# An encoder trunk: gates and latent up-projections in alternation, one summed column in the first norm, one multiplication per settled head

## The chip, the core and the metric

The kernel runs on one core of a Trainium2 chip. A core has engines that work side by side, each through its own list of instructions in order: TensorE (PE) for matrix products, VectorE (DVE) and ScalarE (ACT) for work on elements, GpSimd (POOL), and SyncE (SP), which here issues the transfers (DMAs) from HBM into the on-chip memory (SBUF). Matrix products land in eight accumulation banks (PSUM). Engines wait for one another through semaphores. The metric is the time of one execution on the device in microseconds (us); lower is better.

## What is computed

Two layers of an encoder over 256 positions of width 2048, all in float32. Cut to the parts that the change touches:

```python
h = rmsnorm(x, g_mix[i])
z = h @ w_in[i]
dq, dk, dv, cq, ckv, kr, ga, gb = jnp.split(z, split_at, axis=-1)
# differential attention, 8 heads, two softmax maps each
od = diff_attention(dq, dk, dv, lam)
od = rmsnorm(od, g_subln[i], SUBLN_EPS) * (1.0 - lam_init)
y_diff = od.reshape(b, s, DIFF_WIDTH) @ w_branch_diff[i]
# latent attention, 8 heads
qf = (rmsnorm(cq, g_q_latent[i]) @ w_q_up[i]).reshape(b, s, MLA_HEADS, 192)
q_nope, q_rope = qf[..., :128], apply_rope(qf[..., 128:], cos_m, sin_m)
...
merged = jax.nn.sigmoid(ga) * y_diff + jax.nn.sigmoid(gb) * y_mla
x = x + merged @ w_out[i]
x = x + (silu(gate) * up) @ w_down[i]          # of rmsnorm(x) @ w_gate_up[i]
x = x + sigmoid(rmsnorm(x, g_ple[i]) @ w_ple_gate[i]) * e
```

`ga` and `gb` are the two gates, 2048 columns each. `cq` is the query latent of rank 512, from which `w_q_up` makes 8 heads of 128 plain columns and 64 rotated ones.

## The kernel before

**Products.** Activations are kept transposed, 128 features by 256 positions to a tile, and split into a high and a low part (`ua`, `ub`: 512 columns each). A weight comes by DMA as a piece of eight 128x128 blocks (`piece`, L198), is split into `whi` by ScalarE (L204) and `wlo` by VectorE (`tt`, L82), and for each block `emit` (L245) issues one product of 512 columns with `whi` (L254) and one of 256 columns with `wlo` (L255). `product` (L257) makes one output tile; with 16 blocks (a gate, a key, a query) it takes two pieces. `pair` (L268) makes two output tiles of four blocks each out of one piece: the up-projections. Each output tile takes one of the four banks of `ps_mm` in turn. `joined` (L277) empties a bank: ScalarE copies the right half (L279), VectorE adds the left half to it (L82, `a<-mm,join`). A bank can be used again when that addition is done.

**The order.** The Tile framework places the instructions on the engines with a simulated timeline, following the order in which the program issues them where their operands allow. A dependency of the kind `NO_SYNC` fixes an order on one engine without a semaphore. `after_splits` (L238) has what stands inside issued after the last weight split. `last_block` holds the last L255 product.

**The first norm** (L535 to L538). While x comes in, `squared` (L229) puts the squares of two feature tiles at a time beside each other into one [128, 2, 256] tile and adds these up in `sq0[0]` on VectorE. `norm` (L310) sums over the features with products against a column of ones (L315), one for each sum and half of the positions; with two sums these are four, in two records each. In the second layer it has one sum.

**The differential heads.** `pipelined` (L696) works through eight heads and calls `step` twice for each: 16 steps, each of which moves the generator `beside` (L614) on to its next `yield`. `beside` puts other products between the parts of a head: in steps 1 to 12 the remaining queries and keys, the key up-projections and `shared_key` (L396); in steps 13 to 16 the query up-projections 8, 0, 2 and 10 (8 and 10: the rotated parts of four heads each; 0 and 2: the plain parts of two heads each; two tiles each time), a gate behind 0 and behind 10; then two more gates. `queries_up` (L590) calls `pair` and, for plain parts, splits the joined tile (L288 or L289 on ScalarE, L85 on VectorE), for rotated parts calls `rotated` (L386): a shuffle (L381), two multiplications, an addition, and for each of two heads a conversion on ScalarE (L390) and a half on VectorE (L85). `gate` (L632) multiplies a joined product by the row factor `R`.

**The latent heads.** `pipelined` runs again with `some_gate` (L718) as its step: one gate in each, and ahead of it what `later` (L715) names for that step: the settling of heads 0 to 3 in step 0, `queries_up(4)` in step 2, the settling of heads 4 to 7 in step 4, `queries_up(6)` in step 7. Heads 4 to 7 read the rotated queries that `queries_up(10)` makes; the scores of head 4 are issued after step 6. `mla_weights` (L727) makes scores (L437), exponentials (L450) and normalised weights, `turned` (L454) transposes them (L459), `mla_out` (L736) multiplies with the values (L747).

**Settling** (`settle`, L685). The output of a differential head stands in `od[h]`, 128 positions by two blocks of 128 columns (one per block of positions). The inverse roots of the mean squares are taken for four heads at once (`rsqrt`, L291). Then for each block VectorE multiplies in place with the factor of its position (`ts`, L88) and PE transposes the block (L693).

Of the kernel before, what the change touches and what calls it, by code (L numbers as in the profile page):

```python
# [16 lines left out]
ALU = mybir.AluOpType  # L17
AX = mybir.AxisListType

P = 128  # L20
T = 256
DM = 2048
# [27 lines left out]
NO_SYNC = mybir.DependencyInfo(mybir.DependencyClass.NoSync, mybir.DependencyReason.DATA)  # L50
# [10 lines left out]
def encoder(ctx, tc, x, p, positions, cols, lams, wq, wk, wv, wcq, wckv, wkr, wga, wgb,  # L61
            w_q_up, w_kn, w_v, w_bd, w_bm, w_out, w_gate, w_up, w_down, w_pin, w_pg, w_pin_end, w_pg_end, g_end, rope_c, out):
    nc = tc.nc
    V, A, PE = nc.vector, nc.scalar, nc.tensor
# [13 lines left out]
    def bank(ps=ps_at, tag="at", name="at", shape=(P, 2 * T)):  # L78
        return ps.tile(list(shape), F32, tag=tag, name=name)

    def tt(o, a, b, op):
        return V.tensor_tensor(out=o, in0=a, in1=b, op=op)  # L82
# [4 lines left out]
    def ts(o, a, s1, s2, op0, op1=ALU.bypass):  # L87
        return V.tensor_scalar(out=o, in0=a, scalar1=s1, scalar2=s2, op0=op0, op1=op1)  # L88
# [11 lines left out]
    def operand(t):  # L100
        return t.rearrange("p c t -> p (c t)")
# [4 lines left out]
    def in_turn(u):  # L106
        return u.rearrange("p (c h t) -> p h t c", c=2, h=2)

    def by_parity(row):
        return row.rearrange("p (t c) -> p c t", c=2)  # L110
# [16 lines left out]
    ident = const.tile([P, P], F32, name="ident")  # L127
    make_identity(nc, ident)
    ones = const.tile([P, P], F32, name="ones")
# [99 lines left out]
    def squared(c):  # L229
        for j in range(c // 2, c // 2 + 2):  # L230
            sq0.append(fb(j))
            A.activation(sq0[j], xT[:, 2 * j : 2 * j + 2, :], AF.Square)
            if j:
                tt(sq0[0], sq0[0], sq0[j], ALU.add)

    last_split, last_mm, chores, sq0, step, last_block = [], [], [], [], [], [None]

    def after_splits():  # L238

        stack = ExitStack()  # L240
        for i in last_split:
            stack.enter_context(tc.issue_after(i.ins))
        return stack

    def emit(acc, hi, lo, at, us, first, last, whole):  # L245
        for j, u in enumerate(us):
            s, start, stop = slice((at + j) * P, (at + j + 1) * P), first and j == 0, last and j == len(us) - 1
            t = in_turn(u)
            if whole:
                PE.matmul(acc[:, :T], hi[:, s], t[:, 0], start=start, stop=False)  # L250
                PE.matmul(acc[:, :T], hi[:, s], t[:, 1], start=False, stop=False)
                PE.matmul(acc[:, :T], lo[:, s], t[:, 0], start=False, stop=stop)
            else:
                PE.matmul(acc, hi[:, s], t, start=start, stop=False)  # L254
                last_block[0] = PE.matmul(acc[:, T:], lo[:, s], t[:, 0], start=False, stop=stop)  # L255

    def product(src, us, whole=False):  # L257
# [10 lines left out]
    def pair(src, us):  # L268

        n = len(us)  # L270
        hi, lo = piece(src.rearrange("n p m -> p n m"), 2 * n)
        for j in range(2):
            acc = bank(ps_mm, "mm", "mm")
            emit(acc, hi, lo, j * n, us, True, True, False)
            yield acc

    def joined(acc, o=None):  # L277
        t = scratch("join", 3)
        A.activation(t, acc[:, T:], AF.Copy)  # L279
        o = scratch("a", 4) if o is None else o  # L280
        tt(o, acc[:, :T], t, ALU.add)
        return o
# [8 lines left out]
    def rsqrt(src, n, eps, width):  # L291

        v, y, a = (stat.tile([P, 2 * DH], F32, tag="r" + s, name="r" + s, bufs=2)[:, :width] for s in "vya")
        ts(v, src, 1.0 / n, eps, ALU.mult, ALU.add)
        ts(y.bitcast(I32), v.bitcast(I32), -0.5, 1597463007.0, ALU.mult, ALU.add)
        for _ in range(3):
            stt(a, y, -0.5, y, ALU.mult, ALU.mult)
            tt(a, a, v, ALU.mult)
            stt(y, a, 1.5, y, ALU.add, ALU.mult)
        return y  # L300
# [9 lines left out]
    def norm(sums, n):  # L310

        s = bank()
        for j, a in enumerate(sums):
            for b in range(2):
                PE.matmul(s[:, b : b + 1], by_parity(a)[:, b], ones[:, 0:1], start=j + b == 0, stop=j + b == len(sums))  # L315
        return rsqrt(s[:, 0:2], n, EPS, 2)

    def spread(col):

        s = bank()  # L320
        for b in range(2):
            PE.matmul(s[:, b * P : (b + 1) * P], col[:, b : b + 1].to_broadcast([P, P]), ident, start=True, stop=True)
        row = stat.tile([P, T], F32, tag="row", name="row", bufs=2)
        A.activation(row.rearrange("p (t c) -> p t c", c=2), s[:, :T].rearrange("p (c t) -> p t c", c=2), AF.Copy)
        return row
# [201 lines left out]
    for L in range(DEPTH):  # L527

        steps = values(wv[L], ua, None if L else load)
        for vd in steps:  # L530
            if L == 0 and vd is not None:
                chores.extend(lambda c=c: squared(c) for c in range(0, NC, 4))
                for _ in range(4):
                    next(steps)
                with after_splits():  # L535
                    rcol = norm([sq0[0][:, j, :] for j in range(2)], DM)
                    next(steps)
                    R = spread(rcol)  # L538
                    cos_p, sin_p, cos_m, sin_m = tables()
                    lambdas()  # L540
                break
            if L:
                next(steps)
                rcol = norm([acc], DM)
                next(steps)
                R = spread(rcol)
                break
# [42 lines left out]
        def queries_up(n):  # L590
            for acc in list(pair(w_q_up[L, n : n + 2], cq)):
                if n < MH:
                    qn.append(operand(fa(PLACES[len(qn)], F32R)))
                    split(qn[-1], joined(acc), MLA_SCALE)
                else:
                    if n > MH:
                        qr.append(operand(fc(len(qr) - 2, F32R)))
                    at = qr[len(qr) - 1] if n > MH else qr[ropes[0]]
                    rotated(joined(acc), cos_m, sin_m, at)
                    ropes[0] += 1  # L600
# [13 lines left out]
        def beside():  # L614

            for h in range(2, DH):
                queries_keys(h)
                yield
                if h < 6:
                    keys_up(2 * h - 4)  # L620
                elif h == 7:
                    shared_key(wkr[L], ua, crm, srm)
                yield
            for j, n in enumerate((8, 0, 2, 10)):
                queries_up(n)
                if j % 2:
                    gate(wga, gate_a, next(todo))
                yield
            for _ in range(2):
                gate(wga, gate_a, next(todo))  # L630

        def gate(w, store, n):  # L632
            tt(store(n), joined(product(w[L, n], ua)), R, ALU.mult)
# [12 lines left out]
        todo = iter(range(NC))  # L646
# [7 lines left out]
        od, ods, homes, last_out = [], ub[:8], [], [None]  # L654
# [30 lines left out]
        def settle(h0):  # L685

            rd = rsqrt(ssd[:, 2 * h0 : 2 * h0 + 8], P, SUB_EPS, 8)
            for h in range(h0, h0 + 4):
                t = bank()
                for b in range(2):  # L690
                    o, j = od[h][:, b * P : (b + 1) * P], 2 * (h - h0) + b
                    ts(o, o, rd[:, j : j + 1], None, ALU.mult)
                    PE.transpose(t[:, b * P : (b + 1) * P], o, ident)  # L693
                split(ods[h], t[:, :T], gsub[:, L : L + 1], blocks=True)

        def pipelined(weigh, put, heads, step):  # L696
# [15 lines left out]

        oms = ub[12:] + ub[8:12]
        ahead = iter(range(EARLY))
        later = {0: lambda: settle(0), 2: lambda: queries_up(4), 4: lambda: settle(4), 7: lambda: queries_up(6)}  # L715
        steps = itertools.count()

        def some_gate():  # L718
# [49 lines left out]
        acc, add = stream(ub, f"g_ffn{L}")  # L768
# [5 lines left out]
        R, _, pre = normed_rows(acc, lambda: product(w_gate[L, 0], ub), lambda: product(w_up[L, 0], ub))  # L774
# [5 lines left out]
        for part, (f0, f1) in enumerate(FF_PARTS):  # L780
            for f in range(f0, f1):
                a = pre.pop(0) if pre else joined(product(w_gate[L, f], ub))
                tt(a, a, R, ALU.mult)
                s = scratch("sig", 2)
# [3 lines left out]
                b = pre.pop(0) if pre else joined(product(w_up[L, f], ub))  # L788
# [3 lines left out]
            if last:  # L792
                acc, add = stream(ub, f"g_ple{L}")
# [8 lines left out]
            if part == 1 and L == DEPTH - 1:  # L802
# [7 lines left out]
                hi, lo = piece(w_pin_end, 8)  # L810
                for b in range(2):
                    acc_ = bank(ps_mm, "mm", "mmv")
                    for k in range(2):
                        s = slice(k * 512, (k + 1) * 512)
# [14 lines left out]
        else:  # L829
            acc, add = stream(ua, f"g_mix{L + 1}")  # L830
        for n in range(FM if final else NC):
            a = pre.pop(0) if pre else joined(product(w_pg[L * NC + n], ub))
            tt(a, a, R, ALU.mult)
            s = scratch("sig", 2)
# [4 lines left out]
            if final and n in (3, 5):  # L839
                b = (n - 3) // 2  # L840
                t = bank()
# [6 lines left out]
    for a in range(0, first, 2):  # L848
        m = min(2, first - a)
        hi, lo = piece(w_pg_end[:, a * 512 : (a + m) * 512], 4 * m)  # L850
        for j in range(m):
            s = slice(j * 512, (j + 1) * 512)
# [61 lines left out]
    for i in range(END - 1):  # L914
        o = fb(i).rearrange("p m (n t) -> p (m n) t", t=P)
# [11 lines left out]
    for i, queue in ((1, nc.sync), (0, nc.sync), (2, nc.scalar)):  # L927
        o = operand(fb(3 + i))
# [100 lines left out]
```

## Time and profile before

| what | before |
|---|---|
| median of 3 runs | 2720.53 us (2720.01 to 2720.70) |
| the profiled execution | 2720.81 us |
| its span in the trace | 2719.0 us |
| PE, DVE, ACT busy | 2706.3, 2064.6, 1570.1 us |
| first layer | 0 to about 1360 us |
| differential heads with their steps, first layer | about 106 to 215 us |
| latent heads, first layer | about 216 to 340 us |

All durations come from one profiled execution; the trace's span is 1.8 us shorter than the time of that execution on the device. An engine counts as busy while an instruction of it runs, and instructions of PE overlap, so the step from one start to the next tells more of its pace than the duration of one. A timeline row gives the start, the time taken, the engine, the line, the operation, the tile written and those read, and in square brackets the idle time before it and who ended it. In a row of groups stand the count, the busy time, the mean duration in ns, and the idle time of the engine before it. A row of waits gives who waited for whom, the total, the number and the longest. A row of windows gives the busy time of PE, of PE's weight loads, of DVE, ACT and POOL, the granted PE clock, and the DMA's share and rate.

### The profile page before, as it was taken

How to read it: one execution, taken by the hardware profiler on the slowest of the kernel's cores; microseconds unless marked ns; L12 is line 12 of the kernel's file. 1: busy time of each engine (PE TensorE's matmuls, PEld its weight loads, DVE VectorE, ACT ScalarE, POOL GpSimd, SP SyncE). 2: the span in 40 equal slices, each digit the busy share in tenths (PEclk: the TensorE clock that was granted, in tenths of full speed). 3: DMA queues.
4: the chain of work that ended last, by engine and by line, in shares of the span. 5: the costliest groups of instructions: out<-in, count | busy, mean ns of one | idle time of the engine just before them, and what ended most of it. 6: DMA issues, size and time to landing. Idle time of an engine off the chain costs nothing.

```text
span 2719.0 us, 43648 instructions
## 1 busy us (share of the span) xinstructions
PE 2706.3 (100%) x16608; PEld 2482.9 (91%) x16608; DVE 2064.6 (76%) x3426; ACT 1570.1 (58%) x2562; POOL 1.7 (0%) x9
## 2 busy tenths in 40 slices
PE   9999999999999999999999999999999999999998
PEld 8999999999999999999989899999999999999997
DVE  8899668777667777777869986687776677677777
ACT  7786557565445545555747865565554455455555
POOL 0000000000000000000000000000000000000000
PEclk9999999999999999999999999999999999999999
DMA  7555566666666666666665555666656666666665
GB/s 253 178 166 180 164 201 200 201 200 201 197 205 201 194 201 209 201 203 199 202 200 172 164 180 173 201 201 201 201 200 197 205 202 190 212 200 201 200 199 164
DMA packets 157058, 531.53 MB, mean 195 GB/s; under 512 B 17200, under 2 KB 23472, under 8 KB 156848
## 3 DMA queue, kind: packets, MB, share of 16 engines
q1 hardware_dynamic: 156272, 527.90, 60.5%
q8 instruction: 130, 2.13, 0.3%
q10 hardware_dynamic: 576, 0.85, 0.1%
q14 instruction: 80, 0.66, 0.1%
HBM read 526.58 MB, written 2.10 MB: 194 GB/s over the span
## 4 chain that ended last, share of the span: by engine, by line
PE 98%; DVE 1%; ACT 0%; issue 0%; DMA 0%; SPq 0%; ACTq 0%
PE mm L254 61%; PE mm L255 30%; PE mmv L223 1%; PE mmv L227 1%; PE mmv L226 1%; PE S L437 1%; PE at L459 1%; PE at L674 0%; PE at L747 0%; DVE wlo L82 0%; DVE a L82 0%; DMA w<-in_wv 0%; ACT whi L204 0%; PE at L693 0%; PE mm L409 0%
## 5 line engine op out<-in xcount | busy, mean ns | idle before, releaser
L204 ACT ACTIVATE whi<-w 128x1024 fp32r<-128x1024 f32 (+2 forms) x1024 | 1054.5, 1030 | 1070.0 <-issue 512.5
L82 DVE TENSOR_TENSOR wlo<-w,whi 128x1024 fp32r<-128x1024 f32 (+2 forms) x1024 | 1217.4, 1189 | 574.3 <-ACT whi L204 563.7
L254 PE MATMUL mm<-ub,whi 128*128 128x512 f32 x3904 | 1281.4, 382 | 3.2 <-DVE a L82 3.2
L254 PE MATMUL mm<-ua,whi 128*128 128x512 f32 x3704 | 1222.1, 383 | 0.0
L255 PE MATMUL mm<-ub,wlo 128*128 128x256 f32 x3904 | 1063.2, 273 | 0.0
L255 PE MATMUL mm<-ua,wlo 128*128 128x256 f32 x3704 | 1010.6, 273 | 0.0
L254 PEld LDWEIGHTS mm<-ub,whi 128*128 128x128 f32 x3904 | 737.6, 189 | 105.8 <-DVE a L82 3.8
L254 PEld LDWEIGHTS mm<-ua,whi 128*128 128x128 f32 x3704 | 699.6, 189 | 94.7
L255 PEld LDWEIGHTS mm<-ub,wlo 128*128 128x128 f32 x3904 | 749.5, 192 | 0.4
L255 PEld LDWEIGHTS mm<-ua,wlo 128*128 128x128 f32 x3704 | 711.0, 192 | 2.2 <-DVE wlo L82 0.6
L82 DVE TENSOR_TENSOR a<-mm,join 128x256 f32<-128x256 f32 x418 | 173.8, 417 | 0.1
L279 ACT ACTIVATE join<-mm 128x256 f32<-128x256 f32 x444 | 162.8, 368 | 4.2 <-PE mm L255 4.0
L82 DVE TENSOR_TENSOR xT<-xT,mm 128x256 f32<-128x256 f32 x256 | 106.8, 420 | 33.4 <-PE mm L255 29.3
L82 DVE TENSOR_TENSOR a<-a,row 128x256 f32<-128x256 f32 x204 | 86.1, 424 | 5.8
L288 ACT ACTIVATE ua<-a 128x256 fp32r<-128x256 f32 x120 | 59.1, 492 | 2.6 <-DVE a L82 2.6
L82 DVE TENSOR_TENSOR ua<-a,ua 128x256 fp32r<-128x256 f32 x120 | 55.0, 458 | 1.2 <-ACT ua L288 1.2
L82 DVE TENSOR_TENSOR a<-a 128x256 f32<-128x256 f32 x120 | 51.0, 425 | 4.0
L450 ACT ACTIVATE E<-S,nm 128x256 f32<-128x256 f32 x96 | 44.4, 476 | 12.8 <-DVE nm L448 12.3
L223 PE MATMUL mmv<-whi,ua 128*128 128x512 f32 x132 | 50.6, 384 | 0.4 <-ACT whi L204 0.4
L226 PE MATMUL mmv<-whi,ua 128*128 128x512 f32 x132 | 50.0, 380 | 0.0
L227 PE MATMUL mmv<-wlo,ua 128*128 128x512 f32 x132 | 43.7, 380 | 0.0
L289 ACT ACTIVATE ub<-xT,gcol 128x256 fp32r<-128x256 f32 x64 | 39.5, 618 | 1.7 <-DVE xT L82 1.7
(227 smaller groups left out, 1245.0 us busy)
## 6 DMA issues: line engine op xcount, KB each, us to landing
w<-in_w_gate SPq DMA_DIRECT2D x176, 512.0 KB, 4.7
w<-in_w_up SPq DMA_DIRECT2D x176, 512.0 KB, 4.7
w<-in_w_down SPq DMA_DIRECT2D x128, 512.0 KB, 4.3
w<-in_wga SPq DMA_DIRECT2D x64, 512.0 KB, 3.8
w<-in_wgb SPq DMA_DIRECT2D x64, 512.0 KB, 4.1
w<-in_w_out SPq DMA_DIRECT2D x64, 512.0 KB, 4.7
w<-in_w_pg SPq DMA_DIRECT2D x56, 512.0 KB, 4.7
w<-in_w_down SPq DMA_DIRECT2D x64, 384.0 KB, 3.8
```

Source lines behind the costliest of these rows:

```text
L82: return V.tensor_tensor(out=o, in0=a, in1=b, op=op)
L204: last_split[:] = A.activation(hi, w, AF.Copy), tt(lo, w, hi.bitcast(F32), ALU.subtract)
L223: mm = PE.matmul(bank_, xh, wh, start=first, stop=False)
L226: PE.matmul(bank_, xl, wh, start=False, stop=False)
L227: return PE.matmul(bank_, xh, wl, start=False, stop=last)
L254: PE.matmul(acc, hi[:, s], t, start=start, stop=False)
L255: last_block[0] = PE.matmul(acc[:, T:], lo[:, s], t[:, 0], start=False, stop=stop)
L279: A.activation(t, acc[:, T:], AF.Copy)
L288: return A.activation(hi, src, AF.Copy), tt(lo, src, hi.bitcast(F32), ALU.subtract)
L289: return A.activation(hi, src, AF.Copy, scale=gain), stt(lo, src, gain, hi.bitcast(F32), ALU.mult, ALU.subtract)
L437: mm = PE.matmul(S[:, b, :], q[:, b], k, start=j == 0, stop=j == len(pairs) - 1)
L450: last_exp[0] = A.activation(E[:, b, :].rearrange("p (c t) -> p c t", c=2), by_parity(S[:, b, :]), AF.Exp, bias=nm[:, b : b + 1], accum_ou ...
```

## The change

Four edits, in three parts. (1) `beside` issues, in steps 13 to 16, a gate; the up-projections 8 and a gate; 0; a gate and 2; and then one more gate. `queries_up(10)` is issued in step 3 of the latent heads. While `in_order` is set, the first product of each output tile in `emit` is placed behind the last block of the product before it (no semaphore). Number and size of all products stay as they were. (2) In the first layer one addition on VectorE joins the two columns of sums, and `norm` gets one sum. (3) `settle` multiplies both blocks of a head by one operation of two tensors, the factor broadcast along the columns, and then transposes both.

```diff
@@ -233,7 +233,7 @@
             if j:
                 tt(sq0[0], sq0[0], sq0[j], ALU.add)
 
-    last_split, last_mm, chores, sq0, step, last_block = [], [], [], [], [], [None]
+    last_split, last_mm, chores, sq0, step, last_block, in_order = [], [], [], [], [], [None], [False]
 
     def after_splits():
 
@@ -251,7 +251,9 @@
                 PE.matmul(acc[:, :T], hi[:, s], t[:, 1], start=False, stop=False)
                 PE.matmul(acc[:, :T], lo[:, s], t[:, 0], start=False, stop=stop)
             else:
-                PE.matmul(acc, hi[:, s], t, start=start, stop=False)
+                mm = PE.matmul(acc, hi[:, s], t, start=start, stop=False)
+                if start and in_order[0]:
+                    tc.add_manual_dep(mm.ins, last_block[0].ins.name, NO_SYNC, reason="short products between long ones")
                 last_block[0] = PE.matmul(acc[:, T:], lo[:, s], t[:, 0], start=False, stop=stop)
 
     def product(src, us, whole=False):
@@ -533,7 +535,8 @@
                 for _ in range(4):
                     next(steps)
                 with after_splits():
-                    rcol = norm([sq0[0][:, j, :] for j in range(2)], DM)
+                    tt(sq0[0][:, 0, :], sq0[0][:, 0, :], sq0[0][:, 1, :], ALU.add)
+                    rcol = norm([sq0[0][:, 0, :]], DM)
                     next(steps)
                     R = spread(rcol)
                     cos_p, sin_p, cos_m, sin_m = tables()
@@ -621,13 +624,19 @@
                 elif h == 7:
                     shared_key(wkr[L], ua, crm, srm)
                 yield
-            for j, n in enumerate((8, 0, 2, 10)):
-                queries_up(n)
-                if j % 2:
-                    gate(wga, gate_a, next(todo))
-                yield
-            for _ in range(2):
-                gate(wga, gate_a, next(todo))
+            in_order[0] = True
+            gate(wga, gate_a, next(todo))
+            yield
+            queries_up(8)
+            gate(wga, gate_a, next(todo))
+            yield
+            queries_up(0)
+            yield
+            gate(wga, gate_a, next(todo))
+            queries_up(2)
+            yield
+            gate(wga, gate_a, next(todo))
+            in_order[0] = False
 
         def gate(w, store, n):
             tt(store(n), joined(product(w[L, n], ua)), R, ALU.mult)
@@ -687,10 +696,10 @@
             rd = rsqrt(ssd[:, 2 * h0 : 2 * h0 + 8], P, SUB_EPS, 8)
             for h in range(h0, h0 + 4):
                 t = bank()
+                o, j = od[h].rearrange("p (b t) -> p b t", b=2), 2 * (h - h0)
+                tt(o, o, rd[:, j : j + 2, None].to_broadcast([P, 2, P]), ALU.mult)
                 for b in range(2):
-                    o, j = od[h][:, b * P : (b + 1) * P], 2 * (h - h0) + b
-                    ts(o, o, rd[:, j : j + 1], None, ALU.mult)
-                    PE.transpose(t[:, b * P : (b + 1) * P], o, ident)
+                    PE.transpose(t[:, b * P : (b + 1) * P], o[:, b], ident)
                 split(ods[h], t[:, :T], gsub[:, L : L + 1], blocks=True)
 
         def pipelined(weigh, put, heads, step):
@@ -712,7 +721,7 @@
 
         oms = ub[12:] + ub[8:12]
         ahead = iter(range(EARLY))
-        later = {0: lambda: settle(0), 2: lambda: queries_up(4), 4: lambda: settle(4), 7: lambda: queries_up(6)}
+        later = {0: lambda: settle(0), 2: lambda: queries_up(4), 3: lambda: queries_up(10), 4: lambda: settle(4), 7: lambda: queries_up(6)}
         steps = itertools.count()
 
         def some_gate():
```

## The prediction

> **What bounds the kernel now.** I read the page first: busy time, granted clock, the chain that ended last.
>
> ```profile
> PE 2706.3 (100%) x16608; PEld 2482.9 (91%) x16608; DVE 2064.6 (76%) x3426; ACT 1570.1 (58%) x2562; POOL 1.7 (0%) x9
> PEclk9999999999999999999999999999999999999999
> PE 98%; DVE 1%; ACT 0%; issue 0%; DMA 0%; SPq 0%; ACTq 0%
> ```
>
> TensorE (PE) is the bound: busy 2706.3 of 2719.0 us, at the full clock in all slices, and 98% of the chain. The change removes no large product, so what can be won is what PE waits for, and what small operations cost it. The view of PE's waits lists the first, whole:
>
> ```profile
> PE mm L254 <- DVE a L82: 3.2, 2, 1.6
> PE at L516 <- DVE share L135: 1.1, 1, 1.1
> PE mmv L223 <- ACT whi L204: 0.4, 1, 0.4
> ```
>
> The last two stand at the program's start (warming up, first weights), where nothing changes. The first is two waits of 1.6 us for VectorE (DVE), one in each layer. PE's timeline places them:
>
> ```profile
> 200.99 1.06 PE L674 MATMUL at<-vals,wt 128*128 128x128 f32 x8
> ...
> 205.70 0.27 PE L255 MATMUL mm<-ub,wlo 128*128 128x256 f32 x1
> 207.57 0.48 PE L254 MATMUL mm<-ub,whi 128*128 128x512 f32 x1 [1.60 <-DVE a L82]
> 207.90 0.27 PE L255 MATMUL mm<-ub,wlo 128*128 128x256 f32 x1
> 208.00 0.38 PE L254 MATMUL mm<-ub,whi 128*128 128x512 f32 x1
> ...
> 1555.96 0.27 PE L255 MATMUL mm<-ub,wlo 128*128 128x256 f32 x1
> 1557.84 0.48 PE L254 MATMUL mm<-ub,whi 128*128 128x512 f32 x1 [1.61 <-DVE a L82]
> ```
>
> An L255 product is normally followed 0.11 us later (207.90 to 208.00), so the steps of 1.87 and 1.88 us lose 1.76 and 1.77: **3.53 us**. The operand `ub` says that these are up-projections of queries: `queries_up(2)` and half of `queries_up(10)` run up to 205.70, and the second half waits. It is the fifth product on the four banks of `ps_mm`, so it needs the bank of the gate before the three, whose last block was out at 200.99. VectorE's timeline has the addition that frees it:
>
> ```profile
> 207.10 0.42 DVE L82 TENSOR_TENSOR a<-mm,join 128x256 f32<-128x256 f32 x1
> 207.44 0.41 DVE L85 SCALAR_TENSOR_TENSOR fa<-a,fa 128x256 fp32r<-128x256 f32 x1
> ...
> 1557.37 0.42 DVE L82 TENSOR_TENSOR a<-mm,join 128x256 f32<-128x256 f32 x1
> ```
>
> The bank came free 6.58 us after its product (200.99 to 207.57). The cause is a queue; the table by windows shows it, and the room later:
>
> ```profile
> 190.00:200.00 10.00, 10.00 (x71) 9.02 (x70) 9.59 (x23) 9.09 (x21) 0.00 (x0) 1.00 0.52 169
> 200.00:210.00 10.00, 8.40 (x55) 7.57 (x54) 9.86 (x25) 9.90 (x29) 0.00 (x0) 1.00 0.45 141
> ...
> 250.00:260.00 10.00, 10.00 (x70) 9.37 (x69) 8.81 (x25) 6.07 (x12) 0.00 (x0) 1.00 0.51 171
> 260.00:270.00 10.00, 10.00 (x71) 9.34 (x70) 8.53 (x21) 5.33 (x10) 0.00 (x0) 1.00 0.49 160
> 270.00:280.00 10.00, 10.00 (x67) 9.26 (x66) 7.29 (x14) 5.83 (x12) 0.00 (x0) 1.00 0.49 157
> ```
>
> After the width come PE, PEld, DVE, ACT. From 200 to 210 us VectorE is busy 9.86 and ScalarE 9.90 of 10 us; from 250 to 280 (latent heads) they leave 5.37 and 12.77 us.
>
> **Part 1: gates and short products alternate.** PE's price of a gate:
>
> ```profile
> 209.37 0.48 PE L254 MATMUL mm<-ua,whi 128*128 128x512 f32 x1
> ...
> 214.71 1.06 PE L674 MATMUL at<-vals,wt 128*128 128x128 f32 x8
> ```
>
> A gate of 16 blocks is 5.34 us; an up-projection pair (two products, 8 blocks together) half, 2.67. A bank is wanted again after three other products. Before, PE had pairs 8, 0, a gate, pairs 2, 10: the three between were short ones, 4.0 us, and with 0.8 us of L674 the bank had 4.8 us to come free; it took 6.58, hence the wait of 1.76. After, the row is gate, 8, gate, 0, gate, 2, gate: any three neighbours hold a gate and two halves or more, at least 5.34 + 2.67 = 8.0 us. With a queue as late as today's 6.58 us, 1.4 us are to spare, without counting attention products between. So both waits go: **-3.53 us**. If the queue were over 8 us late, something between 0 and this is won.
>
> Is the queue later or earlier? By groups, apart by shape:
>
> ```profile
> L82 DVE TENSOR_TENSOR wlo<-w,whi 128x1024 fp32r<-128x1024 f32 x925 | 1132.6, 1224 | 527.0 <-ACT whi L204 517.0
> L82 DVE TENSOR_TENSOR a<-mm,join 128x256 f32<-128x256 f32 x416 | 173.0, 417 | 0.1
> ...
> L381 DVE STREAM_SHUFFLE sh<-a 128x256 f32<-128x256 f32 x10 | 4.3, 446 | 0.0
> L85 DVE SCALAR_TENSOR_TENSOR ub<-a,ub 64x256 fp32r<-64x256 f32 x8 | 3.9, 482 | 0.2
> ```
>
> A rope pair (8 or 10): one weight split 1.22, and twice join 0.42, shuffle 0.45, three more like the join, two halves at 0.48: 1.22 + 2 x 3.09 = 7.4 us. Neighbours overlap by 0.08 us (207.10 with 0.42, then 207.44), 14 times: about 6.3 us. A gate: two splits, join, one multiplication, 3.3 us. So a gate gives VectorE 2.0 us of air, a rope pair takes 3.6 to 4.7. The first gate now comes ahead of pair 8, and pair 10 leaves this stretch: not later, I take it.
>
> Pair 10 moves to step 3 of the latent heads, near 255 us, between `queries_up(4)` and the settling of the last four heads. Its work and its one weight DMA are the old ones, later on the same SP queue, whose order is the program's; the gates move ahead by as much. VectorE has 6.3 to 7.4 us to do before the fifth head's scores read it near 280 us: against it stand 5.37 us of idle time and 2.67 us by which PE's own work lengthens the stretch, 8.0. The three products between two uses of a bank hold a gate there too. I cost it at **0**, hidden by gates on PE; without that cover it costs up to 6.3 us less its own 2.67 in each layer.
>
> The pinned order is no semaphore wait: no product starts ahead of the last block of the one before. Behind a late one the whole of PE queues; but `ua`, `cq` and the weights are written ahead of their turn, and no row of PE's waits names them here. **0**.
>
> **Part 2: the first norm.** PE's timeline has it with two sums (first layer) and with one (second layer), each with what follows:
>
> ```profile
> 47.74 0.99 PE L315 MATMUL at<-ones,fb 128*128 128x1 f32 x8
> 48.59 0.46 PE L254 MATMUL mm<-ua,whi 128*128 128x512 f32 x1
> ...
> 1369.34 0.52 PE L315 MATMUL at<-ones,ssq 128*128 128x1 f32 x4
> 1369.72 0.46 PE L223 MATMUL mmv<-whi,ua 128*128 128x512 f32 x1
> ```
>
> 0.85 us against 0.38: -0.47 on PE. The added sum is a 128x256 addition (0.42, like the join) on VectorE, behind the last weight split. PE has other products for that time, but if the norm's stand right there, it waits up to 0.42. Between -0.47 and -0.05 I take **-0.40**, near the full saving: such additions are queued ahead of PE all over this stretch, and no row of PE's waits names one.
>
> **Part 3: settling.** Two multiplications of half a head become one of 256 columns with a broadcast factor.
>
> ```profile
> 260.77 1.66 DVE L88 TENSOR_SCALAR fa<-fa,ry 128x128 f32<-128x128 f32 x8
> ```
>
> 0.21 us each, 0.42 a head; a product of two 128x256 tensors steps by 0.34. Over 16 heads -1.3 us of VectorE. The Trainium skill speaks against it ("VectorE: DVE Perf Modes", The perf-mode tier table): in fp32 an operation with a scalar runs at up to twice the rate of one of two tensors. By that, an estimated 0.13 us a head would be lost instead; in the rows two starts cost more than the slower stream. Either way: VectorE's time, where it has room, **0**. A head's first transpose can start 0.13 us later; if PE waited for that each time it would be +2.1, but no row of PE's waits names a transpose.
>
> One small term stays open: PE pays for changing kind.
>
> ```profile
> 233.74 0.46 PE L254 MATMUL mm<-ua,whi 128*128 128x512 f32 x1
> 234.03 0.27 PE L693 MATMUL at<-ident,fa 128*128 128x128 f32 x1
> 234.06 0.36 PE L255 MATMUL mm<-ua,wlo 128*128 128x256 f32 x1
> 234.25 0.38 PE L254 MATMUL mm<-ua,whi 128*128 128x512 f32 x1
> ```
>
> 0.51 us for a pair of products (5.34 / 16 = 0.33) and a transpose of about 0.10: some 0.08 us a switch. A new order can make a few more or fewer; three per layer are -0.5 to +0.5. **0**.
>
> **Sum.** The profiled execution took 2720.81 us (span 2719.0). 2720.81 - 3.53 - 0.40 = 2716.9. The median of the runs shown, 2720.53, lies 0.28 below it: **2716.6 us**, 0.14% less.
>
> **Rivals.**
> *The waits stay or move.* If one layer's stays, or each at half, 2718.4; if both, only the norm is won: 2720.1. For it: VectorE is at 9.59 of 10 us from 190 on, and the rope pair 8 is still there. Against: 8.0 us of grace for 6.58.
> *Pair 10 is not hidden (the other side).* On VectorE it stands ahead of the normalised weights that the transposes of the next head (L459) need. Within one head, 250 to 270 us, there are 2.66 us of idle time and the 2.67: 5.3 for 6.3, so from a deadline shorter than 20 us PE waits. One us in each layer gives 2718.6; with none of the idle time used, 3.6, it is 2716.6 + 7.2 = 2723.8; with no cover at all, 6.3, 2729.2. From 2.0 us per layer on the kernel is slower than before. Against: the deadline of its own results is near 280.
> The Trainium skill ("TensorE: Matmul & The Clock Gate", Why this matters for your kernels) warns that idle gaps above about 3 us take PE's clock down, so that such a wait would cost more than itself. In the 1.6 us here the clock stayed at 1.00; no run here shows a longer one.
> *More than forecast.* Full norm, fewer switches: 2716.6 - 0.07 - 0.5 = 2716.0, and with a switch saved at each settled pair (8 per layer at most) 2715.3.
>
> **How the numbers follow.** Forecast 0.62 (2716.0 to 2717.4); waits in part or whole 0.23 (2717.4 to 2720.6); pair 10 exposed 0.09, half of it beyond 2726; more than forecast 0.06. The range 2715.2 to 2720.6 leaves out most of the third and a piece of the last. A measurement of this kernel tells about 0.2%, 5.4 us, from no change; all that the change can win, 3.53 + 0.47 + 0.5, is below that. Within 0.2%: 0.89; faster by more (under 2715.1) 0.06; slower by more (over 2726.0) 0.05.
>
> **What would show it.** PE's wait for `DVE a` is gone; PE's window at 200 to 210 us is 10.00; L315 over `fb` is x4; pair 10 stands near 255 us and PE waits neither at L459 nor at L747 up to 285. Wrong would be a new row of over 1 us in PE's waits, a PE window under 10.00 between 250 and 290, or a total that moves by more than 5.4 us, for which no term here has room.

## The result, and the profile after

| | before | after |
|---|---|---|
| median of 22 runs | 2720.42 us (2719.74 to 2721.01) | 2716.18 us (2715.43 to 2717.48) |
| the profiled execution | 2720.81 us, span 2719.0 | 2716.04 us, span 2714.2 |

The ratio is 0.9985, with a 95% interval of 0.9979 to 0.9991: 4.24 us, 0.16% faster. One execution of the kernel before, among those of the last experiment (the copy on VectorE), took 7372.94 us and is left out of the ratio given there. The view of PE's waits of the kernel after, whole (who waited for whom: total, times, longest):

```profile
PE at L518 <- DVE share L135: 1.1, 1, 1.1
PE mmv L223 <- ACT whi L204: 0.8, 1, 0.8
```

The row of the two waits for `DVE a` is gone, and no other has come. What is left stands at the program's start. The table by windows of the kernel after (PE, PE's weight loads, DVE, ACT, POOL, granted clock, DMA), the same stretches as before:

```profile
190.00:200.00 10.00, 10.00 (x70) 8.99 (x69) 9.78 (x21) 8.90 (x27) 0.00 (x0) 1.00 0.60 210
200.00:210.00 10.00, 10.00 (x67) 9.32 (x66) 9.91 (x23) 8.96 (x20) 0.00 (x0) 1.00 0.38 118
250.00:260.00 10.00, 10.00 (x65) 9.24 (x65) 9.94 (x30) 7.12 (x15) 0.00 (x0) 1.00 0.44 146
260.00:270.00 10.00, 10.00 (x68) 9.29 (x66) 9.91 (x23) 5.50 (x10) 0.00 (x0) 1.00 0.57 188
270.00:280.00 10.00, 10.00 (x70) 9.32 (x68) 8.42 (x17) 6.22 (x13) 0.00 (x0) 1.00 0.51 167
```

PE goes from 8.40 to 10.00 in 200 to 210 us. VectorE is as full there as it was (9.91 against 9.86), so the wait did not go because VectorE had less to do. From 250 to 270 us VectorE rose from 8.81 and 8.53 to 9.94 and 9.91: pair 10 is worked off there, and PE stays at 10.00 beside it.

PE's timeline of the kernel after shows the bank of the second gate, and VectorE's timeline the addition that frees it:

```profile
202.59 0.27 PE L257 MATMUL mm<-ua,wlo 128*128 128x256 f32 x1
202.70 1.06 PE L683 MATMUL at<-vals,wt 128*128 128x128 f32 x8
...
211.89 0.38 PE L254 MATMUL mm<-ub,whi 128*128 128x512 f32 x1
```

```profile
208.11 0.42 DVE L82 TENSOR_TENSOR a<-mm,join 128x256 f32<-128x256 f32 x1
```

The gate ends at 202.70. Its addition is the one at 208.11, by the order of the additions. So its bank is free at 208.53 (208.11 + 0.42), 5.8 us later, and the first product of pair 2 wants it at 211.89, 9.2 us later. Before it was free after 6.5 us and wanted after 4.8.

The first norm, in PE's timeline after:

```profile
48.84 0.52 PE L317 MATMUL at<-ones,fb 128*128 128x1 f32 x4
49.22 0.36 PE L257 MATMUL mm<-ua,wlo 128*128 128x256 f32 x1
```

Four records in 0.38 us in place of eight in 0.85. PE reaches them almost five blocks later than before, after the added sum is done (VectorE's timeline after), and does not wait:

```profile
44.83 0.42 DVE L82 TENSOR_TENSOR fb<-fb 128x256 f32<-128x256 f32 x1
```

### The profile page after: what moved, and what is told of

It is laid out like the page before. It is cut to its first block, busy times and chain, and to the rows that moved or that the text cites. A ratio compares the mean times of both kernels' runs of the same rounds, so it can differ in the third digit from the quotient of the medians.

```text
span 2714.2 us, 43619 instructions
## 1 busy us (share of the span) xinstructions
PE 2704.4 (100%) x16604; PEld 2484.0 (92%) x16604; DVE 2064.6 (76%) x3411; ACT 1570.8 (58%) x2562; POOL 1.7 (0%) x9
## 4 chain that ended last, share of the span: by engine, by line
PE 99%; ACT 0%; DMA 0%; SPq 0%; issue 0%; DVE 0%; ACTq 0%
PE mm L254 61%; PE mm L257 31%; PE mmv L227 1%; PE mmv L223 1%; PE mmv L226 1%; PE S L439 1%; PE at L461 1%; PE at L683 1%; PE at L756 0%; PE mm L411 0%; DMA w<-in_wv 0%; PE at L702 0%; PE at L324 0%; ACT L891 0%; ACT fb L939 0%; PE at L317 0%
## 5 line engine op out<-in xcount | busy, mean ns | idle before, releaser
L227 PE MATMUL mmv<-wlo,ua 128*128 128x512 f32 x132 | 43.6, 380 | 0.0
```

The costliest lines, as they stand in the source:

```text
L227: return PE.matmul(bank_, xh, wl, start=False, stop=last)
```

## Where the 4.8 us of the two traces are

The two executions that were profiled differ by 4.77 us, the medians by 4.24. The two waits are 3.53, the norm 0.47. The same product ahead of the norm, the last L227 before it, starts at different times in the two timelines, before:

```profile
47.52 0.38 PE L227 MATMUL mmv<-wlo,ua 128*128 128x512 f32 x1
```

and after:

```profile
47.09 0.38 PE L227 MATMUL mmv<-wlo,ua 128*128 128x512 f32 x1
```

Of the 0.43 us between them 0.20 are there at 10.39 us (before; 10.19 after), behind the first weights, and the rest comes near 28 us, where PE's steps in the trace of before are a little longer. No edit touches the program up to there, and the medians, which differ by half a microsecond less, do not show it: it is put down to chance. What remains, 4.77 - 3.53 - 0.47 - 0.43 = 0.34 us, has the size of four switches of PE between kinds of products at 0.08 us. Counted in the two traces, PE goes from the long products to others and back 125 times before and 117 times after; the transposes of the settling come in 18 groups before and in 12 after. Eight switches fewer would be 0.64 us at that price, so the direction fits and the price is not exact. One place where four transposes now stand together (PE's timeline after):

```profile
229.24 0.38 PE L254 MATMUL mm<-ua,whi 128*128 128x512 f32 x1
229.46 0.60 PE L702 MATMUL at<-ident,fa 128*128 128x128 f32 x4
229.82 0.36 PE L257 MATMUL mm<-ua,wlo 128*128 128x256 f32 x1
```

## The experiments

Times are medians; each is compared with runs of the kernel before on the same chip. They are in groups, by the question.

### Which edit carries the gain

**The norm alone.** Only the added sum and the one-sum norm.

> The kernel before with the first norm's one sum alone. My theory: four product records fewer in the first layer, -0.47 us on PE (0.85 against 0.38 us), both 1.6 us waits for VectorE stay: 2720.0 +- 0.3 us. Rival (PE waits for the added sum): 2720.4 or more, with a row of PE's waits for DVE at the norm.

Measured 2719.93 us against 2720.68, ratio 0.9997 (0.9989 to 1.0006). The waits for `DVE a` stay at 3.2 us in total. The interval holds no change, so the time alone does not show the gain; its size, 0.75 us, is 0.3 more than expected.

**Settling alone.** Only the one multiplication per head.

> The kernel before with the settling by one multiplication alone. My theory: both 1.6 us waits stay; PE saves only switches, three per layer at 0.08 us, so -0.2 to -0.5 us: 2720.1 us. Rival (VectorE's shorter settling is what shortened its queue): the waits go, -3.5 us, 2716.9.

2720.45 against 2720.68, ratio 1.0000 (0.9990 to 1.0009); the two waits are 3.3 us in total. The rival falls: a shorter settling does not shorten the queue in question. The gain of 0.2 to 0.5 us that was expected is too small for these runs.

**The new order alone.** Alternation, pinning and pair 10's move, with norm and settling as before.

> The kernel before with the new order alone (gates and short products alternate and are pinned, pair 10 in the latent heads). My theory: both waits go, -3.5 us, 2716.9 us; no wait of PE in the latent heads. Rival (the three edits share the gain): less than half of it, 2718.7 or more.

2716.80 against 2720.68, ratio 0.9985 (0.9976 to 0.9994); the row of waits for `DVE a` is gone. The order carries 3.88 us, nearly all. The three parts one by one, 0.75 + 0.23 + 3.88 = 4.86, are near the 4.24 of all together.

### What in the order does it

**Pinning alone**, in the old order:

```diff
+            in_order[0] = True
             for j, n in enumerate((8, 0, 2, 10)):
...
             for _ in range(2):
                 gate(wga, gate_a, next(todo))
+            in_order[0] = False
```

> The kernel before, in its old order 8, 0, gate, 2, 10, gate, gate, with the pinning of products alone. My theory: three short products still stand between a gate and the next use of its bank, so both waits stay at 1.4 to 2.0 us: 2720.4 us. Rival (the gain comes from products that no longer mix): the waits go or halve, 2718.6 or less.

2723.11 against 2720.68, ratio 1.0009 (1.0000 to 1.0018), between 2721.12 and 2724.59: outside the time that either theory gave, and slower, though the interval just touches no change. PE's waits of this kernel:

```profile
PE mm L254 <- DVE a L82: 1.8, 2, 0.9
PE at L461 <- DVE E L85: 1.4, 2, 0.7
```

The wait for the bank is halved, and a second one of 0.7 us stands beside it, for the weights `E` of the last differential head that L461 transposes. Together they are 3.2 us, as much as before. So VectorE's queue has two debts to PE in this stretch, and a product that fills one lets the other come up. What else this run showed is told in the last section.

**Pair 10 moved, no alternation, no pinning** (8, 0, gate, 2, gate, gate, gate):

```diff
-            for j, n in enumerate((8, 0, 2, 10)):
+            for n in (8, 0, 2):
                 queries_up(n)
...
-        later = {0: lambda: settle(0), 2: lambda: queries_up(4), 4: lambda: settle(4), 7: lambda: queries_up(6)}
+        later = {0: lambda: settle(0), 2: lambda: queries_up(4), 3: lambda: queries_up(10), 4: lambda: settle(4), 7: lambda: queries_up(6)}
```

> The kernel before with pair 10 moved to step 3 of the latent heads, otherwise in the old order (8, 0, gate, 2, gate, gate, gate), not pinned. My theory (a bank is wanted again after three products, VectorE gives it back some 6.5 us after its product): behind the first gate now stand two halves and a gate, 8.0 us, so both waits go without any alternation: 2717.0 us. Rival (alternation is needed): the waits stay, 2720.4.

2717.83 against 2720.45, ratio 0.9990 (0.9981 to 0.9999). The row for `DVE a` is gone: a gate now follows pair 2, and alternation is not needed for that. A small new row stays:

```profile
PE mm L255 <- DVE wlo L82: 0.6, 2, 0.3
```

Pairs 8 and 0 still stand in a row. The gain is 2.62 us, 1.26 less than that of the whole new order on its chip (3.88); 0.6 of this is the row, the rest was not traced further.

**Alternation with pair 10 kept** (gate, 8, gate, 0, gate, 2, gate, 10):

> The kernel before with the alternation, pinned, but pair 10 kept in the differential heads (gate, 8, gate, 0, gate, 2, gate, 10). My theory: any three products in a row still hold a gate, so both waits go although VectorE has pair 10's 6.3 us there: 2717.0 us. Rival (VectorE's total load in this stretch decides): a wait of 1 us or more in each layer stays, 2718.5 to 2720.5.

2716.53 against 2720.45, ratio 0.9986 (0.9976 to 0.9995), and no wait of PE for VectorE but the one at the start. Pair 10's work on VectorE alone does not make the wait, and with the alternation moving it is not needed.

**The new order without the pinning**:

> The new order alone without the pinning. My theory: the waits are gone as with it, 2716.9 us, give or take some switches (0.08 us each) where blocks of two products mix. Rival (the pinning is needed): a wait of over 0.5 us per layer comes back, 2718 or more.

2716.49 against 2720.45, ratio 0.9985 (0.9976 to 0.9994), no such wait. The gain is 3.96 us, against 3.88 with the pinning: it does nothing here.

**Pair 10 moved, but the short pairs bunched behind one gate**, pinned:

```diff
+            queries_up(8)
+            gate(wga, gate_a, next(todo))
+            yield
+            queries_up(0)
+            queries_up(2)
+            yield
...
```

> The kernel before with pair 10 moved to the latent heads, but the short products bunched behind one gate (8, gate, 0, 2, gate, gate, gate), pinned. My theory: the gate's bank is wanted after three short products again, 4 to 5 us for a VectorE that needs 5.8 to 6.6, so a wait of 0.8 to 1.8 us per layer is back although pair 10's work is gone: 2718.5 to 2720.2. Rival (the load of pair 10 made the wait): no wait, 2717.0.

2719.26 against 2720.45, ratio 0.9995 (0.9986 to 1.0004). PE's timeline of this kernel, and VectorE's:

```profile
199.41 0.27 PE L257 MATMUL mm<-ub,wlo 128*128 128x256 f32 x1
199.52 0.38 PE L254 MATMUL mm<-ub,whi 128*128 128x512 f32 x1
...
204.12 0.39 PE L682 MATMUL at<-vals,wt 128*128 128x128 f32 x2
205.55 0.48 PE L254 MATMUL mm<-ua,whi 128*128 128x512 f32 x1 [1.05 <-DVE a L82]
```

```profile
200.25 0.42 DVE L82 TENSOR_TENSOR a<-mm,join 128x256 f32<-128x256 f32 x1
205.08 0.42 DVE L82 TENSOR_TENSOR a<-mm,join 128x256 f32<-128x256 f32 x1
```

This test says most. Pair 10's work is gone from here, and the wait is back, 1.05 us, in the range that was written down. The expectation named the gate's bank, and it is another that waits. The first gate's bank came free in time (by the order of the additions, the one at 200.25). The bank that is late is that of the first half of pair 0, whose last block is through at 199.52: free at 205.50, 6.0 us later, and wanted after three more halves by the next gate, which starts at 205.55. Three short products between two uses of a bank, and a queue that is 6 us late: the rule held for a bank that is not a gate's too.

### Whose queue it is

**Less for VectorE.** The kernel before without the rotation of pair 8 (about 2.7 us of VectorE per layer left out):

> The kernel before with a part left out: the rotation of pair 8 (shuffle, two multiplications, addition for each of its two tiles), some 2.7 us of VectorE per layer ahead of the late gate. My theory (the wait is VectorE's queue): both waits of 1.6 us go or fall below 0.3 us, 2717 to 2717.5. Rival (ScalarE, 9.90 of 10 us busy, holds the gate's bank): the waits stay above 1 us.

One run, 2719.89 against 2720.62. The waits are 0.9 us each: neither theory. VectorE's addition to the gate starts at the same place as before, 207.11 against 207.10. Its timeline and ScalarE's show why:

```profile
205.17 0.88 DVE L85 SCALAR_TENSOR_TENSOR E<-E,rsum,E 128x256 f32<-128x256 f32 x2
205.97 1.22 DVE L82 TENSOR_TENSOR wlo<-w,whi 128x1024 fp32r<-128x1024 f32 x1
207.11 0.75 DVE L82 TENSOR_TENSOR a<-mm,join 128x256 f32<-128x256 f32 x2
```

```profile
204.39 1.04 ACT L204 ACTIVATE whi<-w 128x1024 fp32r<-128x1024 f32 x1
205.34 0.37 ACT L279 ACTIVATE join<-mm 128x256 f32<-128x256 f32 x1
```

The gate's bank is emptied in two steps, ScalarE's copy and VectorE's addition. ScalarE copies at 205.34, 4.4 us behind the gate (in the kernel before at 204.23, 3.2 us behind). When the copy is done, at 205.71, VectorE is at the last head's weights, and it takes a weight split before the addition. With less to do, VectorE has put these weights ahead of the addition, which gains nothing: ScalarE is late as well, and the order on VectorE is another. The wait is shorter because the transposes of the last head, ready earlier, are done in it, as PE's timeline of this run shows:

```profile
205.81 0.85 PE L460 MATMUL at<-ident,E 128*128 128x128 f32 x4
207.58 0.48 PE L254 MATMUL mm<-ub,whi 128*128 128x512 f32 x1 [0.92 <-DVE a L82]
```

**ScalarE taken out of the way.** The kernel before, with the copy of this one gate on VectorE:

```diff
+        if alone:
+            V.tensor_copy(t, acc[:, T:])
+        else:
+            A.activation(t, acc[:, T:], AF.Copy)
```

> The kernel before, but the first gate of each layer (the one whose bank is waited for) is emptied by VectorE alone: its copy goes from ScalarE to VectorE. In the trace of before ScalarE's copy starts 3.2 us after the gate's last product and VectorE's addition 2.9 us after that. Theory after the run without pair 8's rotation (two queues in a row hold the bank, ScalarE's first): the addition no longer waits for ScalarE, the wait falls below 1.0 us per layer, 2717.5 to 2719.5 us. Rival (VectorE's queue alone decides, as the prediction put it): the waits stay at 1.4 us or more, with 0.3 us of VectorE's work on top, 2720 us or more.

Neither theory holds whole. The wait falls below the 1.0 us that was written down, but the time does not follow: 2720.83 against 2720.27, ratio 1.0002 (0.9992 to 1.0012). PE's timeline of this kernel, and VectorE's:

```profile
200.77 1.06 PE L677 MATMUL at<-vals,wt 128*128 128x128 f32 x8
206.59 0.45 PE L254 MATMUL mm<-ub,whi 128*128 128x512 f32 x1 [0.83 <-DVE a L82]
```

```profile
202.75 0.41 DVE L280 COPY join<-mm 128x256 f32<-128x256 f32 x1
206.02 0.42 DVE L82 TENSOR_TENSOR a<-mm,join 128x256 f32<-128x256 f32 x1
```

The gate ends at 200.77, VectorE copies 2.0 us later, and its addition follows only at 206.02, since VectorE does other work in between. So the bank is free 5.7 us after the gate (206.44), where it took 6.5 before. Taking ScalarE out won 0.9 us of the delay; the rest is VectorE's own queue. PE's waits of this kernel:

```profile
PE mm L254 <- DVE a L82: 1.7, 2, 0.8
PE at L462 <- DVE E L85: 1.2, 2, 0.6
```

It is much the picture of the pinned run: one wait shortened, and PE stands again 2 us later, at the transposes. The kernel before had that second debt too. VectorE's timeline of before has the last head's weights finished at 208.98:

```profile
208.10 0.88 DVE L85 SCALAR_TENSOR_TENSOR E<-E,rsum,E 128x256 f32<-128x256 f32 x2
```

and PE transposes them at 208.99, right behind the half of pair 10 that had waited: without that wait it would have come to them some 1.8 us sooner, before they were ready, and stood there instead. In the kernel after they are finished at 204.20, and PE reads them at 206.22:

```profile
203.33 0.87 DVE L85 SCALAR_TENSOR_TENSOR E<-E,rsum,E 128x256 f32<-128x256 f32 x2
```

```profile
206.22 0.60 PE L461 MATMUL at<-ident,E 128*128 128x128 f32 x4
```

With gates of 5.3 us on PE between the short products, both debts are paid in time there.

**More for VectorE.** The changed kernel with 18 more multiplications behind pair 8:

```diff
             queries_up(8)
+            for _ in range(18):
+                tt(extra, R, R, ALU.mult)
```

> The changed kernel with 18 additional 128x256 multiplications on VectorE behind pair 8, some 6 us per layer. In its trace the latest gate's bank is free 5.8 us after its product and wanted after 9.4 us, 3.6 to spare. My theory: the 6 us use that up, and a wait of up to 2.4 us per layer comes back near 212 us: 2716.2 to 2721. Rival (the queue has no part in it any more): no wait, 2716.2.

One run, 2716.66, no wait. This says nothing: the added operations read only `R`, and the scheduler put them where VectorE had room, from 63.2 us on:

```profile
L82 DVE TENSOR_TENSOR extra<-row x36: 414/423/429, 63.2 to 1392.1; 128x256 f32<-128x256 f32 x36
```

How much later VectorE may get before the wait is back was therefore not measured; the trace of the changed kernel gives 9.2 - 5.8 = 3.4 us of spare for that one bank (the expectation has 9.4 and 3.6).

### Is pair 10 hidden by distance

**Pair 10 in step 6**, just ahead of the scores that read it:

```diff
-        later = {0: lambda: settle(0), 2: lambda: queries_up(4), 3: lambda: queries_up(10), 4: lambda: settle(4), 7: lambda: queries_up(6)}
+        later = {0: lambda: settle(0), 2: lambda: queries_up(4), 4: lambda: settle(4), 6: lambda: queries_up(10), 7: lambda: queries_up(6)}
```

> The changed kernel with pair 10 in step 6 of the latent heads, just ahead of the scores of head 4 that read it. My theory: its cost is hidden only by distance; here some 5 us of VectorE and ScalarE lie between its products and these scores with one gate of 5.3 us on PE beside them, so PE waits 0.5 to 4 us per layer: 2717 to 2724. Rival (place does not matter): 2716.2.

2716.08 against 2720.62, ratio 0.9983 (0.9974 to 0.9993), no wait of PE in the latent heads. My expectation fell. PE's timeline shows the scores of head 4 torn in two, and the transposes of the head before between them:

```profile
278.05 0.50 PE L439 MATMUL S<-fb,fa 128*128 128x256 f32 x3
278.39 0.60 PE L461 MATMUL at<-ident,E 128*128 128x128 f32 x4
...
282.43 0.39 PE L439 MATMUL S<-kr,fc 128*128 128x256 f32 x2
```

The part that needs pair 10 (`fc`) is placed 4 us behind the part that doesn't, with pair 6 and three blocks of a gate in between; pair 10 itself runs from 269.0 to 272.1 us. The order is made anew by the scheduler for each program, and independent products were at hand.

## Why the prediction was right, point by point

- **The bound.** PE is the bound, and only its waits and small costs could be won: shown. The gain of 4.24 us lies within 3.53 + 0.47 + 0.5, which the prediction named as all that can be won. It held that such a change could not be told from none; the 22 runs tell it (0.9979 to 0.9991).
- **Both waits go, -3.53.** Shown by the trace and by the order alone (3.88 us). The rule behind it, a bank is wanted again after three other products, so that a gate should be among them, is borne out by the runs in which a gate follows pair 2 (moved, kept, unpinned: no such wait) and by the bunched run (1.05 us back).
- **What makes the queue late.** This was named in part only. The prediction read the wait as VectorE's. For the larger part it is: with ScalarE out of the way the bank still took 5.7 us, in place of 6.5. But ScalarE's copy comes 3.2 us behind the gate first, and a second debt, the last head's weights, stood right behind the wait. Less work for VectorE won 0.7 us (one run), and by the transposes, not by an earlier bank. So the order of the work in the queues decides, and not its amount alone. The new order works since it gives PE something long to do, not since VectorE gets ahead: VectorE is as full as before (9.91 of 10 us).
- **Pair 10 costs nothing.** Right: PE at 10.00 from 250 to 280 us. The rival that feared for it fell, even at the latest possible place. The prediction also counted on the move to keep VectorE's queue from getting later. It is not needed for that: with pair 10 kept the time is 2716.53. Alone it won 2.62 us (2717.83), since a gate then follows pair 2; the bunched run, with the same move, waits again.
- **The pinned order, 0.** Right in the new order (3.88 us won with it, 3.96 without, each on its chip). In the old one it costs 2.4 us.
- **The norm, -0.40.** 0.47 on PE in the trace, the full saving. By time it is inside the interval.
- **Settling, 0.** Within what can be measured (-0.23 us, interval across no change). On VectorE it saved less than the 1.3 us of the prediction, as the groups by shape show, before and then after:

```profile
L88 DVE TENSOR_SCALAR fa<-fa,ry 128x128 f32<-128x128 f32 x32 | 6.6, 282 | 0.1
```

```profile
L82 DVE TENSOR_TENSOR fa<-fa,ry 128x256 f32<-128x256 f32 x16 | 5.7, 419 | 0.0
```

That is 0.9 us. The prediction's 0.21 us each is 1.66 / 8, which counts the end of the last one in; from the start of the eight to the next operation it is 0.20. The estimate that it drew from the Trainium skill ("VectorE: DVE Perf Modes", The perf-mode tier table), 0.13 us a head lost, did not come: 0.06 a head was won.
- **Switches, 0.** About -0.3 us in the trace, inside the bound of 0.5; with it the sum would have been 2716.3. The forecast gain was 3.93 us from the median of before, the measured one 4.24; the norm in full and the switches make about that difference. That forecast and median come within 0.4 us of each other is in part luck, as the runs of the changed kernel alone spread by 2 us (2715.43 to 2717.48).

## What to carry to other kernels

Where an engine is 99.5% busy, look up its few waits one by one, and ask of each which buffer was wanted, how long after its last use, and how much work of the waiting engine lies in between: here long and short products in turn stretched that time without any engine getting faster. Behind one wait look for the next thing that is late, since a fix of the first may only bring up that one, as in the pinned run and in the one with the copy on VectorE. And where a scheduler orders the program, an experiment that adds or moves work must be read from the trace first: here the added multiplications went elsewhere than the edit meant, and behind the late pair 10 the scheduler moved the scores that needed it.

## What the hardware showed unexpectedly

In the run with pinning alone, the two waits in the first layer lie close together: between 205.34 and 208.07 us PE did four transposes and nothing else. PE's timeline and the table by windows of that run (the last but two figures of a row are the granted clock):

```profile
205.23 0.27 PE L257 MATMUL mm<-ub,wlo 128*128 128x256 f32 x1
206.20 0.94 PE L461 MATMUL at<-ident,E 128*128 128x128 f32 x4 [0.70 <-DVE E L85]
208.07 0.48 PE L254 MATMUL mm<-ub,whi 128*128 128x512 f32 x1 [0.92 <-DVE a L82]
```

```profile
207.00:209.00 2.00, 1.08 (x7) 0.88 (x6) 2.00 (x5) 1.93 (x6) 0.00 (x0) 0.92 0.10 23
209.00:210.00 1.00, 1.00 (x4) 0.82 (x4) 0.97 (x2) 0.18 (x1) 0.00 (x0) 0.50 0.90 283
210.00:211.00 1.00, 1.00 (x5) 0.91 (x4) 0.94 (x3) 0.75 (x1) 0.00 (x0) 0.50 0.63 221
211.00:212.00 1.00, 1.00 (x5) 0.82 (x4) 1.00 (x4) 0.97 (x3) 0.00 (x0) 0.50 0.66 205
212.00:214.00 2.00, 2.00 (x14) 1.84 (x13) 2.00 (x6) 0.14 (x1) 0.00 (x0) 0.97 0.40 147
```

From about 209 to 212 us the granted clock is 0.50, and pairs of products take 0.64 us in place of 0.33. Three microseconds at half speed are some 1.5 us lost, as much as the waits themselves. In the second layer of the same run the same two waits (0.67 and 0.92 us) left the clock at 1.00, as the single waits of 1.6 us in the kernel before did, so one trace does not show what decides. The Trainium skill ("TensorE: Matmul & The Clock Gate", Part 4: PE-mode transpose) says that transposes do not count as work for the gate in the way that products do. The first layer fits that without proving it: the idle time alone was 0.70 + 0.92 us, and the time without a product 2.7. The spread of this kernel's runs, 2721.12 to 2724.59 us, is wider than that of any other kernel here (3.5 us against 2.2 at most). That the clock falls in some executions and not in others, or in both layers, would explain it. The mean granted clock that each run lists fits: it is 0.998 in three of the eleven runs of this kernel, the slowest among them, and 0.999 in the other eight and in every run of the other kernels that was counted. Only one run was profiled, so it is not shown.
